# Mixer-0 norm and memory requests, and the state space's dq requests, issued in other places of a weight-streaming trunk

## The chip, the cores and the metric

One core of a Trainium2 chip runs the whole program. The metric is device time in microseconds; the kernel before takes 2868.22 us, the median of three runs (2866.78 to 2868.61).

## The reference

Two decoder layers over x of 256 tokens by 2048, batch 1, with 256 memory rows. Each layer is a token mixer, a cross-attention to the memory and a squared-ReLU MLP of width 8192, each on an RMS norm of x and added to x; a last RMS norm ends it. Mixer 0 is a gMLP, mixer 1 a complex-diagonal state space with a gated output. All is float32.

```python
def chunked_gmlp(h, w_in, b_in, ln_g, ln_b, w_s, b_s, w_out):
    z = jax.nn.gelu(h @ w_in + b_in, approximate=False)
    u, v = jnp.split(z, 2, axis=-1)
    v = layer_norm(v, ln_g, ln_b)
    v = v.reshape(bsz, seq // CHUNK, CHUNK, A_HEADS, A_HEAD_DIM)
    w = jnp.where(causal[None], w_s, 0)
    s = jnp.einsum('hts,bnshd->bnthd', w, v) + b_s   # one 128x128 matrix per head
    return (u * s.reshape(bsz, seq, A_WIDTH)) @ w_out

def s5_glu(h, w_in, lam, log_dt, bm, cm, d_skip, w_out, b_out):
    u = (h @ w_in).reshape(bsz, seq, B_GROUPS, B_GROUP)
    # per group: state s_t = lam_bar * s_(t-1) + b_bar u_t (64 complex), y = Re(c s) + d u
    y = jax.nn.gelu(y, approximate=False)
    val, gate = jnp.split(y @ w_out + b_out, 2, axis=-1)
    return val * jax.nn.sigmoid(gate)

# memory: k, v = rms_norm(mem, g_mem) @ w_kv, in both layers
```

## The kernel before

Weights are not resident: each matrix comes from HBM in chunks of 512 KB, 128 partitions by 1024 float32. `wload` (L118) requests a chunk on SP's queue into one of four `wraw` buffers. `split` (L101, L102) divides it into a rounded part `whi` (a ScalarE cast) and the remainder `wlo` (a VectorE subtraction), three buffers each. TensorE then takes twelve matmuls per chunk (L145 to L147): activation high part by `whi`, high by `wlo`, low by `whi`. Nearly all of TensorE's work has this form, or its transposed one (L163, L165).

Other work is put between the chunks by a plan. `at(d, fn)` runs a function d chunks later, `tick` at the end of each chunk runs what is due, and takes one step of the list `side` at every `every`-th chunk with a priority `lag` lower. A scheduler then sets each engine's order by priority; on the chip each engine works its list in that order, and a DMA request is an instruction of the engine that issues it. Buffers come from pools: a tile of a tag waits until the last reader of the buffer it takes is done.

The stages of the first mixer, `gmlp`: `features` loads x transposed in pieces (`memc`, two buffers), `zin(n)` makes one of eight column tiles of z with a bias row (`bc`, L111, one row broadcast to 128 partitions, 256 KB, requested on POOL's queue), the first four being v. `mixing` loads w_s as four pieces (`wsr`), masks them on POOL and splits them. `ln(j, t)` normalizes v: L362 subtracts the mean and multiplies by ln_g, L364 scales and adds ln_b. Each pair (ln_g, ln_b) is requested by `ln` at t = 0. b_in, ln_g, ln_b and w_s share the two buffers of the tag `bc`. `gate` and `turn` multiply by the mixed v and transpose. The output projection follows, and behind its first tile `mem_stats` loads the memory in four pieces on POOL's queue (L252, tag `memc`) and sums squares on ScalarE (L176), from which `rstd_mem` is made.

In the state space, `s5`, four column tiles n of u = h @ w_in are made. From each come chunk inputs (transposes, L894), own responses with `pq` (L908), carries (VectorE), and outputs with `dq` (L956) and `qq` (L962). The matrices pq, dq and qq were written to HBM by a preparation that runs beside the MLP of the first layer; they come back as tiles of 512 KB (L854) on POOL's queue, four of each per n, with four buffers per name. Before the first tile the four pq of n = 0 are requested; `follow(n)` puts the others into the plan.

## Time and profile before

| what | us |
|---|---|
| median of three runs | 2868.22 |
| profiled execution, own time | 2870.24 |
| its span, first to last instruction | 2868.5 |
| TensorE busy | 2818.8 (98%) |
| VectorE busy | 1831.0 (64%) |
| ScalarE busy | 1333.9 (47%) |
| POOL busy | 205.6 (7%) |

The mean granted clock of TensorE is 0.996 of full speed. In the rows below, PE is TensorE, DVE VectorE, ACT ScalarE, POOL GpSimd, SP the engine that only issues requests; a suffix q is a request put in a queue. Times are from the start of the span. A number in square brackets at a row's end is the idle time of that engine before the instruction, with what ended it. A lone time after a tile's name is the time from request to landing.

### The profile page before, as it was taken

How to read it: one execution, taken by the hardware profiler on the slowest of the kernel's cores; microseconds unless marked ns; L12 is line 12 of the kernel's file. 1: busy time of each engine (PE TensorE's matmuls, PEld its weight loads, DVE VectorE, ACT ScalarE, POOL GpSimd, SP SyncE). 2: the span in 40 equal slices, each digit the busy share in tenths (PEclk: the TensorE clock that was granted, in tenths of full speed). 3: DMA queues.
4: the chain of work that ended last, by engine and by line, in shares of the span. 5: the costliest groups of instructions: out<-in, count | busy, mean ns of one | idle time of the engine just before them, and what ended most of it. 6: DMA issues, size and time to landing. Idle time of an engine off the chain costs nothing.

```text
span 2868.5 us, 39577 instructions
## 1 busy us (share of the span) xinstructions
PE 2818.8 (98%) x15238; PEld 2362.5 (82%) x15238; DVE 1831.0 (64%) x2548; ACT 1333.9 (47%) x1714; POOL 205.6 (7%) x384
## 2 busy tenths in 40 slices
PE   8999999999999999999999999999999999999998
PEld 6778888888888888888877788888888888888886
DVE  5655655576778878787567567555556555555565
ACT  5444544444544444444555445444454444344443
POOL 1000000000022222222011000000000000000000
PEclk9999999999999999999999999999999999999999
DMA  7766656557677777777689866656566666666665
GB/s 260 221 197 190 200 174 177 176 171 231 197 216 211 225 222 214 220 221 212 217 248 273 233 203 212 184 173 185 169 187 187 192 190 189 192 186 191 190 189 154
DMA packets 180461, 579.55 MB, mean 202 GB/s; under 512 B 37440, under 2 KB 39664, under 8 KB 179504
## 3 DMA queue, kind: packets, MB, share of 16 engines
q1 hardware_dynamic: 140864, 509.67, 58.7%
q0 software_dynamic: 39264, 67.29, 8.6%
q8 instruction: 119, 1.95, 0.3%
q14 instruction: 70, 0.57, 0.1%
q10 hardware_dynamic: 144, 0.07, 0.0%
HBM read 553.88 MB, written 22.94 MB: 201 GB/s over the span
## 4 chain that ended last, share of the span: by engine, by line
PE 88%; DMA 5%; DVE 3%; issue 2%; ACT 1%; POOL 0%; SPq 0%; DVEq 0%; ACTq 0%; POOLq 0%
PE acc L163 23%; PE acc L165 12%; PE acc L146 8%; PE acc L570 8%; PE acc L147 8%; PE acc L569 8%; PE acc L145 8%; PE acc L568 8%; DVE wlo L102 1%; PE ps L504 1%; PE ps L448 1%; DMA wraw<-in_b_w_in 1%; DMA Kd<-kd 1%; PE ps L214 1%; DMA wraw<-in_a_w_in 1%
## 5 line engine op out<-in xcount | busy, mean ns | idle before, releaser
L102 DVE TENSOR_TENSOR wlo<-wraw,whi 128x1024 fp32r<-128x1024 f32 x952 | 1164.1, 1223 | 847.6 <-ACT whi L101 845.7
L101 ACT CAST whi<-wraw 128x1024 fp32r<-128x1024 f32 x952 | 1000.9, 1052 | 1290.8 <-PE acc L163 401.1
L163 PE MATMUL acc<-act,whi 128*128 128x512 f32 x3072 | 1083.0, 396 | 0.3 <-ACT whi L101 0.3
L165 PE MATMUL acc<-act,wlo 128*128 128x256 f32 x3072 | 865.0, 282 | 2.6 <-DVE wlo L102 2.6
L163 PEld LDWEIGHTS acc<-act,whi 128*128 128x128 f32 x3072 | 576.1, 188 | 133.5 <-issue 1.6
L165 PEld LDWEIGHTS acc<-act,wlo 128*128 128x128 f32 x3072 | 580.4, 189 | 7.9 <-DVE wlo L102 4.5
L145 PE MATMUL acc<-whi,act 128*128 128x512 f32 x1248 | 492.6, 395 | 12.7 <-ACT whi L101 11.2
L146 PE MATMUL acc<-wlo,act 128*128 128x512 f32 x1248 | 491.2, 394 | 12.4 <-DVE wlo L102 12.4
L147 PE MATMUL acc<-whi,act 128*128 128x512 f32 x1248 | 489.2, 392 | 0.3 <-DVE act L102 0.3
L569 PE MATMUL acc<-wlo,hh 128*128 128x512 f32 x992 | 389.0, 392 | 0.0
L568 PE MATMUL acc<-whi,hh 128*128 128x512 f32 x992 | 388.8, 392 | 0.0
L570 PE MATMUL acc<-whi,hl 128*128 128x512 f32 x992 | 388.6, 392 | 0.0
L146 PEld LDWEIGHTS acc<-wlo,act 128*128 128x128 f32 x1248 | 236.3, 189 | 64.8 <-DVE wlo L102 17.6
L145 PEld LDWEIGHTS acc<-whi,act 128*128 128x128 f32 x1248 | 235.7, 189 | 64.7 <-ACT whi L101 13.8
L147 PEld LDWEIGHTS acc<-whi,act 128*128 128x128 f32 x1248 | 236.2, 189 | 48.4 <-DVE act L102 0.7
L570 PEld LDWEIGHTS acc<-whi,hl 128*128 128x128 f32 x992 | 186.3, 188 | 40.3 <-issue 1.6
L569 PEld LDWEIGHTS acc<-wlo,hh 128*128 128x128 f32 x992 | 186.3, 188 | 40.2 <-issue 1.0
L568 PEld LDWEIGHTS acc<-whi,hh 128*128 128x128 f32 x992 | 186.3, 188 | 39.7 <-issue 0.4
L819 POOL DMA_DIRECT2D Kd<-kd x128 | 72.4, 581 | 188.8 <-issue 176.7
L101 ACT CAST hh<-r 128x512 fp32r<-128x512 f32 x64 | 39.5, 617 | 23.0 <-DVE r L534 22.8
L552 DVE SCALAR_TENSOR_TENSOR x<-acc,r,x 128x512 f32<-128x512 f32 x62 | 43.7, 746 | 8.6 <-PE acc L570 8.6
L176 ACT ACTIVATE junk<-x 128x512 f32<-128x512 f32 x56 | 35.3, 630 | 21.1 <-DVE x L545 13.5
(288 smaller groups left out, 1661.3 us busy)
## 6 DMA issues: line engine op xcount, KB each, us to landing
wraw<-in_f_w_up SPq DMA_DIRECT2D x256, 512.0 KB, 4.4
wraw<-in_f_w_down SPq DMA_DIRECT2D x256, 512.0 KB, 4.4
wraw<-in_a_w_in SPq DMA_DIRECT2D x64, 512.0 KB, 4.7
wraw<-in_x_w_q SPq DMA_DIRECT2D x64, 512.0 KB, 3.7
wraw<-in_x_w_k SPq DMA_DIRECT2D x64, 512.0 KB, 3.7
wraw<-in_x_w_v SPq DMA_DIRECT2D x64, 512.0 KB, 3.7
wraw<-in_x_w_o SPq DMA_DIRECT2D x64, 512.0 KB, 3.7
wraw<-in_b_w_out SPq DMA_DIRECT2D x64, 512.0 KB, 4.4
```

Source lines behind the costliest of these rows:

```text
L101: self.nc.scalar.copy(out=hi, in_=src)
L102: self.nc.vector.tensor_tensor(out=lo, in0=src, in1=hi.bitcast(F32), op=ALU.subtract)
L145: nc.tensor.matmul(out[t], ah[:, kt, sl], hi[:, kk, :], start=st, stop=False)
L146: nc.tensor.matmul(out[t], ah[:, kt, sl], lo[:, kk, :], start=False, stop=False)
L147: nc.tensor.matmul(out[t], al[:, kt, sl], hi[:, kk, :], start=False, stop=en)
L163: nc.tensor.matmul(acc[:, f, :], hi[:, kk, sl], both[:, kt].rearrange("p a s -> p (a s)"), start=st, stop=False, skip_group_check=True)
L165: nc.tensor.matmul(acc[:, f, 0:S], lo[:, kk, sl], ah[:, kt, :], start=False, stop=en, skip_group_check=True)
L552: nc.vector.scalar_tensor_tensor(out=xc, in0=acc[:, t, :], scalar=r2[:, t:t + 1], in1=xc, op0=ALU.mult, op1=ALU.add)
L568: nc.tensor.matmul(acc[:, t, :], ah[:, kt % 4, sl], hi[:, kk, :], start=st, stop=False)
L569: nc.tensor.matmul(acc[:, t, :], ah[:, kt % 4, sl], lo[:, kk, :], start=False, stop=False)
L570: nc.tensor.matmul(acc[:, t, :], al[:, kt % 4, sl], hi[:, kk, :], start=False, stop=en)
L819: nc.gpsimd.dma_start(out=self.Kd[q // 2][:, :, q % 2, t], in_=kd[32 * t:32 * t + 16])
```

## The change

The bias rows of `zin` get a tag of their own, `bz`, with two buffers, and are requested at the start of the column tile instead of at its activation. The x_t pieces and the memory pieces share a tag `u` of five buffers with the tiles u. `ln` no longer requests its rows: `affine(j)` does, the first ahead of all steps and each following one as a step of its own after pair j's second, with a step at every second chunk instead of every third. The memory pieces are requested on SP's queue behind a weight, one at every second chunk of the output projection's second tile, with the row statistics in a function of their own eight chunks in. In the state space the four dq of n = 0 are requested right behind the four pq of n = 0, and no longer from `follow(0)`.

```diff
--- before.py
+++ after.py
@@ -106,8 +106,8 @@
         a = self.act.tile([P, KT, 2, S], F32R, name="act")
         return a[:, :, 0, :], a[:, :, 1, :], a
 
-    def bc(self, pool, src):
-        t = pool.tile([P, NB], F32, name="bc")
+    def bc(self, pool, src, tag="bc", bufs=None):
+        t = pool.tile([P, NB], F32, name="bc", tag=tag, **({"bufs": bufs} if bufs else {}))
         self.nc.gpsimd.dma_start(out=t, in_=src.rearrange("(o n) -> o n", o=1).broadcast_to([P, NB]))
         return t
 
@@ -248,9 +248,17 @@
         nc = self.nc
         ss = self.new_ss()
         for j in range(NCH):
-            m = pool.tile([P, 2, NB], F32, name="memc")
-            self.tc.keep_in_program_order(nc.gpsimd.dma_start(out=m, in_=self.a["mem"][j]))
-            self.sumsq(m, ss, j)
+            def piece(j):
+                m = pool.tile([P, 2, NB], F32, name="memc", tag="u", bufs=5)
+                with self.tc.issue_after(self.fed):
+                    nc.sync.dma_start(out=m, in_=self.a["mem"][j])
+                self.sumsq(m, ss, j)
+
+            self.at(2 * j, lambda j=j: piece(j))
+        self.at(2 * NCH, lambda: self.mem_rows(ss))
+
+    def mem_rows(self, ss):
+        nc = self.nc
         self.rstd_mem = self.rstd(ss, "rstd_mem", self.const)
         self.rows_mem = self.const.tile([P, 2, P], F32, name="rows_mem")
         pt = self.ps([P, 2, P])
@@ -279,7 +287,7 @@
             ss = self.new_ss()
 
             def features(j):
-                xt = gp.tile([P, 4, S], F32, name="memc")
+                xt = gp.tile([P, 4, S], F32, name="memc", tag="u", bufs=5)
                 for h in range(0, 4, 2):
                     nc.sync.dma_start(out=xt[:, h:h + 2], in_=a["x_t"][j][:, h:h + 2])
                     if j == 0 and h == 0:
@@ -305,22 +313,21 @@
             bs = gp.tile([P, KT], F32, name="bs", bufs=1)
 
             def zin(n, out):
-                nonlocal rstd
+                b = self.bc(gp, a["a_b_in"][n * NB:(n + 1) * NB], "bz", 2)
                 acc = self.gemm_tok(hT, a["a_w_in"], n, raw=first)
                 if rstd is None:
                     self.flush()
                     self.lag = 100
                     for k in range(NCH):
                         self.at((1, 3, 4, 6)[k], lambda k=k: tokens(k))
-                    self.at(7, lambda: activate(n, out, acc))
+                    self.at(7, lambda: activate(n, out, acc, b))
                 else:
-                    activate(n, out, acc)
-
-            def activate(n, out, acc):
+                    activate(n, out, acc, b)
+
+            def activate(n, out, acc, b):
                 nonlocal rstd
                 if rstd is None:
                     rstd = self.rstd(ss, "rstd")
-                b = self.bc(gp, a["a_b_in"][n * NB:(n + 1) * NB])
                 for t in range(2):
                     nc.vector.scalar_tensor_tensor(out=out[:, t, :], in0=acc[:, t, :], scalar=rstd[:, t:t + 1],
                                                    in1=b, op0=ALU.mult, op1=ALU.add)
@@ -354,9 +361,10 @@
 
             lnb = {}
 
+            def affine(j):
+                lnb[j] = [self.bc(gp, a[k][j * NB:(j + 1) * NB]) for k in ("a_ln_g", "a_ln_b")]
+
             def ln(j, t):
-                if t == 0:
-                    lnb[j] = [self.bc(gp, a[k][j * NB:(j + 1) * NB]) for k in ("a_ln_g", "a_ln_b")]
                 lg, lb = lnb[j]
                 vc = v[:, t, j, :]
                 nc.vector.scalar_tensor_tensor(out=vc, in0=vc, scalar=mv[:, t, 0:1], in1=lg,
@@ -366,8 +374,12 @@
                 v4 = vc.rearrange("p (h d) -> p h d", h=4)
                 self.split(vh[:, 4 * j:4 * j + 4, t, :], vl[:, 4 * j:4 * j + 4, t, :], v4)
 
-            self.side += [lambda j=j, t=t: ln(j, t) for j in range(NCH) for t in range(2)]
-            self.every = 3
+            affine(0)
+            for j in range(NCH):
+                self.side += [lambda j=j: ln(j, 0), lambda j=j: ln(j, 1)]
+                if j + 1 < NCH:
+                    self.side += [lambda j=j: affine(j + 1)]
+            self.every = 2
             usT = self.new_act()
 
             def gate(j, u):
@@ -396,16 +408,15 @@
                     kt = 4 * j + 2 * hp
                     self.split(usT[0][:, kt:kt + 2, :], usT[1][:, kt:kt + 2, :], pt)
 
-            us = [gp.tile([P, 2, NB], F32, name="u", bufs=4) for _ in range(NCH)]
+            us = [gp.tile([P, 2, NB], F32, name="u", bufs=5) for _ in range(NCH)]
             for j in range(NCH):
-                if j == 3:
-                    self.every = 1
                 zin(j, us[j])
                 if j:
                     self.at(1, lambda j=j: gate(j - 1, us[j - 1]))
                     self.at(3, lambda j=j: turn(j - 1, us[j - 1]))
             self.at(2, lambda: gate(NCH - 1, us[NCH - 1]))
             self.at(4, lambda: turn(NCH - 1, us[NCH - 1]))
+            self.every = 1
             acc0 = self.gemm_tok(usT, a["a_w_out"], 0, kts=range(12), last=False)
             self.flush()
 
@@ -981,7 +992,8 @@
                 for i in range(4):
                     if n + 1 < NCH:
                         self.at(4, lambda i=i: fetch("pq", n + 1, i))
-                    self.at(6 + i // 2 * 2, lambda i=i: fetch("dq", n, i))
+                    if n:
+                        self.at(6 + i // 2 * 2, lambda i=i: fetch("dq", n, i))
                     self.at(6 + i // 2 * 2, lambda i=i: fetch("qq", n, i))
                 self.at(3, lambda: inputs(n))
                 self.at(4, lambda: own(n))
@@ -994,8 +1006,9 @@
                 self.at(15, lambda: outputs(n, 1))
                 self.at(17, lambda: features(n))
 
-            for i in range(4):
-                fetch("pq", 0, i)
+            for nm in ("pq", "dq"):
+                for i in range(4):
+                    fetch(nm, 0, i)
             for n in range(NCH):
                 acc = self.gemm_tok(hT, a["b_w_in"], n)
                 if n == 0:
```

On POOL, in the first mixer, these are the rows from the first norm pair to the last bias. Before (a_ln_g and a_ln_b are the norm's rows, a_b_in the bias, in_mem the memory):

```order
L111 DMA bc<-in_a_ln_g 128x512
L111 DMA bc<-in_a_ln_b 128x512
L111 DMA bc<-in_a_ln_g 128x512
L111 DMA bc<-in_a_ln_b 128x512
L111 DMA bc<-in_a_b_in 128x512
L111 DMA bc<-in_a_ln_g 128x512
L111 DMA bc<-in_a_ln_b 128x512
L111 DMA bc<-in_a_b_in 128x512
L111 DMA bc<-in_a_ln_g 128x512
L111 DMA bc<-in_a_ln_b 128x512
L111 DMA bc<-in_a_b_in 128x512 x2
L252 DMA memc<-in_mem 128x1024 x4
```

After:

```order
L111 DMA bc<-in_a_ln_g 128x512
L111 DMA bc<-in_a_ln_b 128x512
L111 DMA bc<-in_a_b_in 128x512 x4
L111 DMA bc<-in_a_ln_g 128x512
L111 DMA bc<-in_a_ln_b 128x512
L111 DMA bc<-in_a_ln_g 128x512
L111 DMA bc<-in_a_ln_b 128x512
L111 DMA bc<-in_a_b_in 128x512
L111 DMA bc<-in_a_ln_g 128x512
L111 DMA bc<-in_a_ln_b 128x512
L111 DMA bc<-in_a_b_in 128x512
```

Before, four biases stand ahead of the first row shown (two of them ahead of the mixing weights); now it is two, and four more follow the first norm pair at once. The memory requests are gone from this queue, and no bias stands between the second and the third norm pair.

On POOL, at the head of the state space, where the first matrices are read back (Kd, Pd, Qd are the HBM copies). Before:

```order
L854 DMA pq<-Pd_5524 128x1024
L854 DMA pq<-Pd_5525 128x1024
L854 DMA pq<-Pd_5526 128x1024
L854 DMA pq<-Pd_5527 128x1024
L919 MEMSET vv 128x2x16
L854 DMA dq<-Kd_5556 128x1x1024
L854 DMA qq<-Qd_5540 128x1024
L854 DMA dq<-Kd_5557 128x1x1024
L854 DMA qq<-Qd_5541 128x1024
L854 DMA dq<-Kd_5558 128x1x1024
```

After:

```order
L865 DMA pq<-Pd_5524 128x1024
L865 DMA pq<-Pd_5525 128x1024
L865 DMA pq<-Pd_5526 128x1024
L865 DMA pq<-Pd_5527 128x1024
L865 DMA dq<-Kd_5556 128x1x1024
L865 DMA dq<-Kd_5557 128x1x1024
L865 DMA dq<-Kd_5558 128x1x1024
L865 DMA dq<-Kd_5559 128x1x1024
L930 MEMSET vv 128x2x16
L865 DMA qq<-Qd_5540 128x1024
L865 DMA qq<-Qd_5541 128x1024
L865 DMA qq<-Qd_5542 128x1024
```

The four dq stand directly behind the four pq, in front of the memset of vv; the four qq stay behind it, and the pairs of dq and qq no longer alternate.

On ScalarE, at the first mixer's end, the sums of squares of the memory pieces (junk,ss<-memc) and the weight casts (whi) around them. Before:

```order
L327 ACTIVATE u<-u 128x1024
L101 CAST whi<-wraw 128x1024
L176 ACTIVATE junk,ss<-memc 128x512 x2
L101 CAST whi<-wraw 128x1024
L176 ACTIVATE junk,ss<-memc 128x512 x2
L101 CAST whi<-wraw 128x1024
L101 CAST act<-ps 128x2x256 x2
L176 ACTIVATE junk,ss<-memc 128x512 x3
L101 CAST whi<-wraw 128x1024
L176 ACTIVATE junk,ss<-memc 128x512
L101 CAST whi<-wraw 128x1024 x4
```

After:

```order
L176 ACTIVATE junk,ss<-memc 128x512 x2
L101 CAST whi<-wraw 128x1024 x4
L176 ACTIVATE junk,ss<-x 128x512 x2
L101 CAST whi<-wraw 128x1024
L223 ACTIVATE act<-ps,gcol 128x256 x2
L176 ACTIVATE junk,ss<-memc 128x512 x2
L223 ACTIVATE act<-ps,gcol 128x256 x2
L176 ACTIVATE junk,ss<-memc 128x512
L101 CAST whi<-wraw 128x1024
L176 ACTIVATE junk,ss<-memc 128x512 x2
L101 CAST whi<-wraw 128x1024
L176 ACTIVATE junk,ss<-memc 128x512
```

Three casts lay between the first sum of squares and the last, and now seven; the sums stand later, in the output projection, between activations of the next norm.

## Rows read from the trace of the kernel before

**Rows 1.** The page: engines' busy time, and a costly group of instructions.
```profile
PE 2818.8 (98%) x15238; PEld 2362.5 (82%) x15238; DVE 1831.0 (64%) x2548; ACT 1333.9 (47%) x1714; POOL 205.6 (7%) x384
...
L146 PE MATMUL acc<-wlo,act 128*128 128x512 f32 x1248 | 491.2, 394 | 12.4 <-DVE wlo L102 12.4
```

**Rows 2.** Timeline of ScalarE, an undisturbed stretch: start, length, instruction, idle before.
```profile
97.92 1.05 ACT L101 CAST whi<-wraw 128x1024 fp32r<-128x1024 f32 x1 [1.67 <-PE acc L147]
```

**Rows 3.** Windows: busy time of the engines, granted clock, DMA share, GB/s.
```profile
0.00:25.00 25.00, 15.15 (x52) 10.97 (x53) 13.19 (x23) 14.99 (x25) 2.42 (x9) 1.00 0.79 275
60.00:70.00 10.00, 8.68 (x37) 6.40 (x35) 6.43 (x9) 4.62 (x6) 3.73 (x6) 1.00 0.70 220
130.00:160.00 30.00, 23.67 (x100) 18.35 (x99) 20.76 (x26) 12.73 (x15) 3.81 (x8) 0.94 0.57 174
160.00:190.00 30.00, 25.92 (x112) 20.42 (x111) 15.78 (x31) 15.50 (x28) 1.53 (x3) 0.94 0.71 232
1366.00:1394.00 28.00, 28.00 (x130) 23.27 (x129) 15.27 (x17) 13.40 (x19) 1.72 (x5) 1.00 0.81 272
1441.00:1480.00 39.00, 33.17 (x149) 26.31 (x148) 21.23 (x39) 18.72 (x34) 5.90 (x11) 1.00 0.99 275
1460.00:1490.00 30.00, 24.17 (x160) 18.73 (x159) 13.06 (x16) 17.43 (x34) 2.12 (x4) 0.94 0.95 301
1500.00:1510.00 10.00, 8.33 (x48) 6.51 (x50) 9.57 (x27) 7.32 (x17) 0.00 (x0) 1.00 0.59 167
1530.00:1545.00 15.00, 12.42 (x56) 10.16 (x55) 11.19 (x17) 10.27 (x24) 0.00 (x0) 0.89 1.03 254
```

**Rows 4.** Timeline of VectorE in the layer norm.
```profile
129.46 0.75 DVE L362 SCALAR_TENSOR_TENSOR v<-v,mv,bc 128x512 f32<-128x512 f32 x1 [2.65 <-DMA bc<-in_a_ln_g]
...
151.23 0.75 DVE L364 SCALAR_TENSOR_TENSOR v<-v,rv,bc 128x512 f32<-128x512 f32 x1 [4.65 <-DMA bc<-in_a_ln_b]
```

**Rows 5.** The broadcast rows (tile bc) before 260: request to landing.
```profile
DMA to landing us min/median/max: 4.3/5.3/8.5
```

**Rows 6.** Timeline of POOL in the layer norm.
```profile
123.63 0.54 POOL L111 DMA_DIRECT2D bc<-in_a_ln_g  x1 [2.66 <-DVE v L364]
...
145.73 0.54 POOL L111 DMA_DIRECT2D bc<-in_a_ln_b  x1 [7.02 <-DVE v L362]
```

**Rows 7.** Timeline of ScalarE at the memory rows.
```profile
176.75 0.63 ACT L176 ACTIVATE junk<-memc 128x512 f32<-128x512 f32 x1 [2.76 <-DMA memc<-in_mem]
```

**Rows 8.** Tile memc (x_t and memory pieces) before 260: request to landing.
```profile
DMA to landing us min/median/max: 3.0/5.9/9.2
```

**Rows 9.** Timeline of POOL in the state space.
```profile
1441.24 0.65 POOL L854 DMA_DIRECT2D dq<-Kd  x1 [73.51 <-DVE x L552]
```

**Rows 10.** DMA issues of 1362 to 1376: tiles, queue, KB each, median us to landing.
```profile
wraw<-in_f_w_down SPq DMA_DIRECT2D x5, 512.0 KB, 6.5
pq<-Pd POOLq DMA_DIRECT2D x4, 512.0 KB, 10.2
```

**Rows 11.** DMA issues of 1440 to 1480.
```profile
wraw<-in_b_w_in SPq DMA_DIRECT2D x12, 512.0 KB, 10.7
dq<-Kd POOLq DMA_DIRECT2D x4, 512.0 KB, 21.0
```

**Rows 12.** Timeline of TensorE in the state space, the first tile's transposes.
```profile
1479.18 1.30 PE L894 MATMUL ps<-ident,u 128*128 128x128 f32 x8 [4.13 <-ACT u L883]
```

**Rows 13.** The mixing weights (tile wsr): counts and durations; request to landing.
```profile
L101 ACT CAST wsh<-wsr x4: 620/620/622, 56.6 to 69.5; 128x512 fp32r<-128x512 f32 x4
L102 DVE TENSOR_TENSOR wsl<-wsr,wsh x4: 680/692/693, 57.2 to 70.4; 128x512 fp32r<-128x512 f32 x4
...
DMA to landing us min/median/max: 3.8/4.0/4.4
```

**Rows 14.** Timeline of SP in the start.
```profile
15.91 1.38 SPq L118 DMA_DIRECT2D wraw<-in_a_w_in  x3
```

**Rows 15.** Timeline of ScalarE in the start.
```profile
22.07 1.04 ACT L101 CAST whi<-wraw 128x1024 fp32r<-128x1024 f32 x1 [2.27 <-DMA wraw<-in_a_w_in]
```

## The prediction

> **What bounds the kernel now.** The page comes first: TensorE holds work for 98% of the span, while VectorE has 64% and ScalarE 47% [rows 1]. So the kernel is a stream of weight chunks through TensorE, and the change can pay only where TensorE stands still or runs at a lower clock. A chunk is twelve matmuls; in an undisturbed stretch ScalarE's cast of one takes 1.05 us and stands 1.67 us before it [rows 2], so chunks come every 2.72 us and matmuls start 0.227 us apart, while the page gives each 394 ns because they overlap [rows 1]. A gap shown as idle is therefore about 0.17 us longer in lost time than the number beside it.
>
> The windows view shows where TensorE stands still [rows 3]. The loss of a stretch is its length less the busy time, plus 0.17 per gap, plus busy time times (1 minus the granted clock); a mean of 0.94 is a mixture of full speed and the lower of the two levels.
> - 60 to 70 (the mixing weights are cast): 1.32 idle, three gaps, full clock: 1.8 us.
> - 130 to 160 (layer norm of the first mixer): 6.33 idle, four gaps, clock 0.94 (1.4): 8.4 us.
> - 160 to 190 (statistics of the memory rows): 4.08 idle, three gaps, clock 0.94 (1.6): 6.2 us.
> - 1460 to 1490 (state space, first tile): 5.83 idle, four gaps, clock 0.94 (1.5): 8.0 us.
> - 1500 to 1510 (second tile): 1.67 and 0.17: 1.8 us. 1530 to 1545 (third tile): 2.58 idle, 0.17, clock 0.89 (1.4): 4.2 us.
>
> Together 30 us, about 1% of the time. The timelines of the engines then give the cause of each. In the layer norm TensorE's second matmul of a chunk waits for VectorE's wlo, the costliest such wait of the page [rows 1], and VectorE, which takes its instructions in order, stands before the norm's first or second operation for a weight row that was requested late: 2.65 us in the earliest of four such places and 4.65 in the last [rows 4]. These rows take 4.3 to 8.5 us from request to landing [rows 5]; POOL requests them only when an operation on an earlier row of the tag is over [rows 6]. At the memory rows ScalarE stands twice before a sum of squares, 2.76 us the second time [rows 7], until the DMA of the rows lands, up to 9.2 us after its request [rows 8]; the weight cast is behind it in its queue. In the state space POOL waits 73.51 us for the last MLP down projection's residual and then issues eight 512 KB requests, four dq and four qq, back to back [rows 9]; from then on the DMA engines are busy for 0.99 of 39 us and still move only 275 GB/s [rows 3], a weight chunk, which took 6.5 us to land beside the four pq requests [rows 10], takes 10.7 [rows 11], and at the end the transposes of the first tile stand 4.13 us [rows 12].
>
> **The change, part by part.** The sum is made against the profiled execution, 2870.24 us (span 2868.5 and 1.7 around it), which lies 2.0 above the median of 2868.22.
>
> *Mixing weights.* w_s no longer shares buffers with b_in, so POOL has no wait ahead of its first two loads, and select, cast and subtract of all four pieces move from 51 to 70 us to the first 25. The 1.8 us go: -1.8. In the start the same four casts (0.62) and four subtracts (0.69) [rows 13] stand ahead of the weight casts 4 and 7. TensorE is already idle for 9.85 of the first 25 us [rows 3], waiting on transfers, and that covers the 5.2 us of added work as long as the data are there. Two things pull apart: 1 MB more must land there (at the 275 GB/s of this stretch [rows 3], 3.8 us, the upper end with a little wait, +4), and the fourth weight request, now issued at 15.91 because SP stood behind an x_t piece without a buffer [rows 14], can go out with five buffers at once; the 2.27 us that ScalarE waits for that chunk [rows 15] may go, of which I allow 1.5. I take +0.8, the middle being 1.2 and the nearer row being ScalarE's.
>
> *Layer norm.* Norm pair j+1 is now its own step ahead of pair j's use, and b_in has buffers of its own. In POOL's order b_in goes in front and the norm rows follow each other. Pair 2's weight, requested at 123.63 [rows 6] behind a b_in on the same tag, goes when that b_in went, some 3 us earlier. The last pair waits for operations of earlier pairs that, counted along the changed order, end near 131.7 and 134, where the last bias was requested at 145.73 [rows 6]. With the worst landing of 8.5 us they are there at 140.2 and 142.6; VectorE stood ready for the last bias at 151.23 - 4.65 = 146.6 [rows 4]. So all four waits fall. What is late next is the second pair, still bound by its buffers, and the steps of the norm now come every second chunk instead of every third. I leave 0.8 (from 0 to 2.1, a fourth of the stretch's 8.4, if one of the four waits comes back): -7.6.
>
> *Memory rows.* Four requests leave POOL's queue for SP's, spaced over six chunks of the output projection, into five buffers; counted along ScalarE's order, the sums of squares follow their requests by two chunks for the first piece and four to six for the others. The stretch has 0.71 of the DMA in use at 232 GB/s [rows 3]. Each 512 KB piece delays the weights behind it on the queue by some 1.7 us (at the 301 GB/s that flowed in 1460 to 1490 [rows 3]), and there are two chunks, 5.4 us, for each: 1.05 MB of weights and 0.52 of rows in 5.4 us are 290 GB/s, just under what flowed there. What is left over is 0.2 (0 to 1.4, a third of the idle time now): -6.0. The Trainium skill ("Trainium Kernel Development and Optimization", Key Constraints) says that requests issued by SP, ScalarE and POOL run on the same 16 DMA engines, so that another issuer only saves issue time. By that the move buys nothing in bandwidth, and the saving rests on spacing and buffers alone; the sum here counts none for the queue.
>
> *State space, first tile.* The four dq requests now stand behind the four pq, ahead of the vv memset, and their buffers wait only for TensorE work of the preparation: issue near 1367.6 instead of 1441 to 1445. At 1440 four requests are left of eight, 2.1 MB instead of 4.2. The weights need one chunk in 2.72 us, 193 GB/s. The 8.0 us go, but for 0.8 (0 to 3; the second tile, with no such burst, still loses 1.8): -7.2.
>
> *Third tile.* TensorE's transposes for it stand ten matmuls (2.3 us) later in the changed order; against the 2.75 us gap most of it goes and with it part of the lower clock: -2.8 (-4.2 to 0). The second tile's place is unchanged: 0.
>
> *New burst at 1366.* Four pq requests alone bring the weights' landing to 6.5 us [rows 10], and TensorE has no gap in 1366 to 1394 [rows 3]. Eight requests at 1441 brought 10.7 [rows 11] and the 8.0 us. The new burst is eight again, but with the fast pq first (they land in 10.2 us, dq in 21.0 [rows 10, 11]), in a stage where ScalarE has less beside the casts. Ends: 0 (as with pq alone) and +6 (three quarters of what eight cost at 1441). I take +3. In 1440 to 1480 twelve weight chunks were requested beside eight requests of POOL, of the same 512 KB, so neither queue held the other up for long [rows 11]. The Trainium skill ("DMA: Bandwidth & Descriptors", Queues, rings and completion order) states that each engine takes the queues with work in turn, packet by packet. By it dq's 2.1 MB would take half of 275 GB/s for 15 us, the weights fall behind by 15 x (1 - 137/193) = 4.4 us, and with 6.5 us or so of landing that is what stopped TensorE at 1441: the upper half of the range. The trace agrees as far as the counts go: twelve chunks against eight pieces, not one queue first.
>
> **Sum:** -1.8 + 0.8 - 7.6 - 6.0 - 7.2 - 2.8 + 3 = -21.6. 2870.2 - 21.6 = 2848.6, less the 2.0: 2846.6 us.
>
> **Rivals.**
> 1. The burst only moves. dq at 1367 stops TensorE as it did at 1441, and what the third tile loses stays. For it: the weights' landing of 10.7 under eight requests. Against: pq alone shows no gap, and here half the bytes move 75 us ahead. The state space then gives nothing: -21.6 + 7.2 + 2.8 - 3 = -14.6 from the gMLP, 2853.6.
> 2. Another request is late in the first mixer: ScalarE stands before the memory pieces again, now that weights and rows share one queue, or VectorE before the second norm pair. For it: 290 GB/s asked against 301 seen at best. Against: four to six chunks of lead for three pieces, and two, 5.4 us, for the first against a median landing of 5.9 [rows 8], with ScalarE 1.67 us ahead at each cast [rows 2]. Half of the 13.6 us returns: 2853.4.
> 3. Slower. ScalarE stands in the start before the casts of w_s: the second pair is requested only after the first is subtracted, and each stands ahead of weight casts. If each of the four pieces lands as late as the slowest memory row (9.2 us [rows 8]), one after the other, the price is 4 x (9.2 + 0.62 + 0.69) = 42.0 us, less the 9.85 that TensorE stands there anyway: 32.2, and the sum is -22.4 + 32.2 = +9.8: 2878.0. It decides once the start costs over 22.4 us. Against: w_s landed in 4.0 us where it is loaded now [rows 13], and its requests are issued two at a time.
> 4. The edit does not free dq: its requests wait for the residual, as now, and hold POOL. Nothing but POOL is behind them, so the state space is as before and the gMLP gains: 2853.6 again.
>
> **How the numbers follow.** Forecast 0.62, with its own range 2840 to 2853; rivals 1 and 4 together 0.19; rival 2 0.10; rival 3 0.04; several small things at once that eat it 0.05, at 2860 to 2868. For the range I take the low end from the terms' better ends (start -1.5, burst 0, third tile -4.2: 2840, and 2 more for the clock) and the high end from rivals 1, 2 and 4 with the start at +4 and 4 us more of leftover: 2838 to 2862. What a measurement can tell from no change is 0.2%, 5.7 us: faster needs less than 2862.5. Faster 0.88, within 0.2% 0.08, slower 0.04.
>
> **What would show it.** Right: in 130 to 190 no DVE wait on a norm row and no ScalarE wait on memory rows above 1 us, TensorE busy above 29.5 of each 30; dq issued near 1367; the first tile's transposes waiting under 1.5 us; weights landing in 8 to 11 us around 1375 to 1390 with at most two gaps. Wrong: a gap in 1370 to 1395 of more than 6 us in sum (rival 1), or a start whose 25th microsecond holds fewer than 48 matmul records against 52 [rows 3] (rival 3).

## The result and the profile after

| | before | after |
|---|---|---|
| median, us | 2867.5 (4 runs, 2866.42 to 2868.61) | 2849.49 (4 runs, 2847.75 to 2852.07) |
| ratio to before | 1 | 0.9938, 95% interval 0.9921 to 0.9955 |
| profiled execution, us | 2870.24 | 2848.29 |
| its span, us | 2868.5 | 2846.5 |

The change makes the kernel 18.0 us faster by the medians and 22.0 by the two profiled executions. The forecast was 2846.6, in a range of 2838 to 2862. One run of a later kernel (the last but one below) took 4682.58 us at a granted clock of 0.556 and is left out of its median.

The windows of after, in the columns of [rows 3]. The stretches from 1346 on are shifted by some 20 us against before.

```profile
0.00:25.00 25.00, 15.04 (x50) 10.69 (x51) 15.32 (x25) 15.35 (x26) 7.15 (x16) 1.00 0.89 307
60.00:70.00 10.00, 10.00 (x45) 8.29 (x45) 5.53 (x7) 4.26 (x5) 0.00 (x0) 1.00 0.77 216
130.00:160.00 30.00, 29.03 (x138) 24.04 (x137) 21.30 (x27) 14.06 (x16) 1.07 (x2) 1.00 0.74 223
160.00:190.00 30.00, 30.00 (x143) 25.16 (x142) 16.58 (x19) 12.72 (x14) 0.00 (x0) 1.00 0.59 173
1346.00:1374.00 28.00, 28.00 (x128) 23.06 (x127) 12.77 (x14) 12.26 (x17) 4.76 (x9) 1.00 1.01 270
1374.00:1390.00 16.00, 14.25 (x62) 10.50 (x61) 9.50 (x12) 8.69 (x15) 0.00 (x0) 1.00 0.88 238
1441.00:1471.00 30.00, 29.81 (x195) 24.45 (x194) 18.10 (x26) 19.04 (x36) 2.10 (x4) 1.00 0.70 229
1481.00:1491.00 10.00, 8.34 (x111) 6.23 (x109) 7.75 (x13) 6.35 (x15) 2.08 (x4) 1.00 0.70 199
1506.00:1521.00 15.00, 11.49 (x51) 8.65 (x50) 12.68 (x21) 9.00 (x21) 0.00 (x0) 0.88 1.02 245
```

The three stretches of the first mixer, which lost 1.8, 8.4 and 6.2 us, now lose 0, 1.1 and 0, and the clock is whole again. The memory rows no longer fall into the third of them: they are requested from 204.93 to 220.63 and summed from 210.8 on, and nothing is lost there. TensorE's work in the start is unchanged (15.04 busy, against 15.15), with 307 GB/s instead of 275. The first state space tile (1441 to 1471) loses 0.2 where it lost 8.0. Two things are on the other side: a new loss at 1374 to 1390, 1.75 us idle, and the third tile (1506 to 1521), which is idle 3.51 us where it was 2.58 [rows 3]. The first tile's transposes, which waited 4.13 us in [rows 12]:

```profile
1456.56 1.09 PE L905 MATMUL ps<-ident,u 128*128 128x128 f32 x8 [0.19 <-ACT u L894]
```

The four requests of dq on POOL in after, where [rows 9] has 1441.24 and 73.51 us of waiting; then the DMA issues of 1350 to 1382 in after, beside [rows 10, 11].

```profile
1348.31 1.87 POOL L865 DMA_DIRECT2D dq<-Kd  x3
1350.89 0.58 POOL L865 DMA_DIRECT2D dq<-Kd  x1 [0.71 <-DMA Pd<-po]
```

```profile
wraw<-in_f_w_down SPq DMA_DIRECT2D x9, 512.0 KB, 11.9
dq<-Kd POOLq DMA_DIRECT2D x2, 512.0 KB, 32.0
```

dq is requested at once, and in the MLP the weights now land as late (11.9 us) as they did at 1441 (10.7).

To see where the 22.0 us come from I added, over all neighbouring starts of TensorE's matmuls, what goes beyond the usual distance, for each stretch of both traces. 26 to 130: 2.4 before, 0 after. 130 to 260: 14.7 and 1.1. 1300 to 1400: 0 and 2.5. First tile: 7.3 and 0.4. Second: 1.8 and 1.8. Third: 4.1 and 5.3. The start: 5.9 and 6.1. Between 520 and 1300, which the change does not touch, 4.1 and 2.6. The whole is 44.3 and 23.8, 20.5 us of the 22.0. Each count is of one execution. In the traces of the other runs, counted the same way, a stretch with the same code differs by one to five us, so a difference of a microsecond or two in one stretch says little by itself.

### The profile page after: what moved, and what is told of

It reads as the page before. It is cut to its first block, busy times and chain, and to the rows that moved or that the text cites. A ratio compares the mean times of both kernels' runs of the same rounds, so it can differ in the third digit from the quotient of the medians.

```text
span 2846.5 us, 39576 instructions
## 1 busy us (share of the span) xinstructions
PE 2811.6 (99%) x15238; PEld 2359.5 (83%) x15238; DVE 1830.3 (64%) x2548; ACT 1333.4 (47%) x1714; POOL 204.0 (7%) x380
## 4 chain that ended last, share of the span: by engine, by line
PE 92%; DMA 3%; DVE 2%; ACT 1%; issue 1%; SPq 0%; POOL 0%; DVEq 0%; ACTq 0%; POOLq 0%
PE acc L163 25%; PE acc L165 13%; PE acc L146 9%; PE acc L145 9%; PE acc L147 9%; PE acc L581 8%; PE acc L580 8%; PE acc L579 8%; PE ps L515 1%; DMA wraw<-in_f_w_down 1%; PE ps L459 1%; DVE wlo L102 1%; PE ps L214 1%; DMA wraw<-in_b_w_in 1%; DMA wraw<-in_f_w_up 1%
## 5 line engine op out<-in xcount | busy, mean ns | idle before, releaser
L830 POOL DMA_DIRECT2D Kd<-kd x128 | 72.4, 580 | 178.9 <-issue 166.7
```

What stands on the lines that cost most here:

```text
L830: nc.gpsimd.dma_start(out=self.Kd[q // 2][:, :, q % 2, t], in_=kd[32 * t:32 * t + 16])
```

## The experiments

Ratios are to the kernel before, run on the same chip (medians of 2867.5 to 2868.1 there).

**The first mixer's part alone.** after without the state space edit:

```diff
-            for nm in ("pq", "dq"):
-                for i in range(4):
-                    fetch(nm, 0, i)
+            for i in range(4):
+                fetch("pq", 0, i)
...
-                    if n:
-                        self.at(6 + i // 2 * 2, lambda i=i: fetch("dq", n, i))
+                    self.at(6 + i // 2 * 2, lambda i=i: fetch("dq", n, i))
```

> The whole change without its state space edit: the four dq of the first tile are requested with the qq again, as before. My theory: the first mixer and the state space give their gains independently. By the trace of after, TensorE lost 17.1 us less than before between 26 and 260 us; so 2867.5 - 16 = 2851.5 (2849 to 2854), and the state space shows the old picture: first tile's transposes stand about 4 us, weights land in 10 to 13 us. Rival: the state space carries the gain, as dq stands apart from qq; then this comes out at 2857 or above.

2853.88 us, ratio 0.9955 (0.9940 to 0.9969). The first tile's transposes wait as before, and weights land in 11.3 us:

```profile
1462.65 1.09 PE L905 MATMUL ps<-ident,u 128*128 128x128 f32 x8 [3.91 <-ACT u L894]
```

**The state space's part alone.** The same edit the other way round, made in the kernel before.

> The kernel before with the state space edit alone: the four dq of the first tile requested right behind the four pq. My theory: the first tile's 7 us go and 2.5 us come at the new burst beside the MLP, and the third tile keeps its loss; 2867.5 - 4 = 2863.5 (2861 to 2866). Rival: the state space pays as forecast, with the third tile (10 us less there, 3 at the burst): 2860.5 or lower. Second rival: the burst moved and nothing is gained: 2867.

2865.13 us, ratio 0.9991 (0.9981 to 1.0001): a gain that timing alone hardly separates from none. The trace shows both sides of it: the first tile's loss is gone, and near 1395 TensorE now loses 5.4 us in sum, most of it in front of the MLP's last transposes:

```profile
1394.79 0.33 PE L214 MATMUL ps<-ident,x 128*128 128x128 f32 x1 [2.54 <-DVE x L552]
```

The two parts add up: 0.45% and 0.09% against 0.62% of the whole, inside the intervals. Most of the gain is the first mixer's.

**Memory rows on POOL, all at one point, into five buffers.**

```diff
...
-            self.at(2 * j, lambda j=j: piece(j))
-        self.at(2 * NCH, lambda: self.mem_rows(ss))
...
+            m = pool.tile([P, 2, NB], F32, name="memc", tag="u", bufs=5)
+            self.tc.keep_in_program_order(nc.gpsimd.dma_start(out=m, in_=self.a["mem"][j]))
+            self.sumsq(m, ss, j)
```

> The changed kernel with the memory rows requested as before, all four at one point on POOL's queue and their sums of squares at once, but into the five shared buffers instead of two. Theory spacing: the requests in one burst are what made ScalarE stand before the sums, so a good part of the loss of before (6 us between 160 and 190) is back: 2849.5 + 4 = 2853.5 (2851 to 2856). Theory buffers: the loss came from two buffers that made the last two requests wait for the first sums; with five the loss is 1 us at most: 2850.

2850.48 us, ratio 0.9939 (0.9920 to 0.9958). The window 160 to 190 of this run, and the four requests on POOL:

```profile
160.00:190.00 30.00, 30.00 (x143) 25.16 (x142) 17.06 (x20) 12.57 (x13) 0.53 (x1) 1.00 0.65 210
```

```profile
149.85 0.53 POOL L252 DMA_DIRECT2D memc<-in_mem  x1
158.63 0.54 POOL L252 DMA_DIRECT2D memc<-in_mem  x1 [8.25 <-ACT whi L101]
182.77 0.53 POOL L252 DMA_DIRECT2D memc<-in_mem  x1 [23.60 <-ACT whi L101]
201.37 0.53 POOL L252 DMA_DIRECT2D memc<-in_mem  x1 [18.07 <-ACT junk L176]
```

TensorE is never idle in the window, and the gain is kept on POOL's queue: the new queue did not make it. Whether the spacing did is not shown, because the four requests did not come as a burst. As the five buffers came free they went out over 51 us, and the sums of squares stand at 199.6 to 206.9, where they stood at 166.7 to 178.3 before the change, so that ScalarE waits 0.72 us for one piece at most.

**Mixing weights late.** One tag, so that they wait for the biases' buffers:

```diff
-                wr = gp.tile([P, 4, P], F32, name="wsr", tag="bc", bufs=2)
+                wr = gp.tile([P, 4, P], F32, name="wsr", tag="bz", bufs=2)
```

> The changed kernel with the mixing weights on the bias tag, so that they wait for the biases' buffers as before and are masked and split near 50 to 70 us. My theory: the 2.4 us of TensorE between 60 and 70 come back (in part, since biases and norm rows no longer share the tag), and the start gains nothing, as it lost nothing: 2851.5 (2849 to 2854). Rival: the casts in the start cost as much as they save; then the first 26 us lose 2 us less and the time stays at 2849.5.

2853.07 us, ratio 0.9953 (0.9938 to 0.9968). Between 26 and 130 us 2.6 us are lost again, of which

```profile
87.44 0.50 PE L146 MATMUL acc<-wlo,act 128*128 128x512 f32 x1 [1.51 <-DVE wlo L102]
```

is the largest. The pieces are requested later here than before the change (59.02 to 78.93, against 51.45 to 64.66). The start loses 6.6 us, against 6.1 in after and 6.7 to 8.3 in the nine other runs with the hoist. So the hoist is worth its 2.4 us; that it costs the start nothing is not shown.

**The burst spaced.** The first tile's dq on SP's queue:

```diff
...
-            for nm in ("pq", "dq"):
-                for i in range(4):
-                    fetch(nm, 0, i)
+            def ahead_dq(i):
+                with tc.issue_after(self.fed):
+                    fetch("dq", 0, i, nc.sync)
+
+            for i in range(4):
+                fetch("pq", 0, i)
+                self.at(8 + 3 * i, lambda i=i: ahead_dq(i))
```

> The changed kernel with the four dq of the first tile on SP's queue behind the 8th, 11th, 14th and 17th weight of the state space's input projection (about 1430 to 1455), instead of behind pq in one burst beside the MLP. My theory: the loss of 2.5 us near 1375 goes, the weights there land as before the change (7 us at most), and the four pieces, one in 8 us, cost nothing: 2847 (2844.5 to 2849). Rival: dq costs its transfer wherever it stands, now beside qq of 1423 and pq of 1459: a gap of 2 us or more appears between 1430 and 1470 and the time stays at 2849.5 or rises to 2853.

2848.07 us, ratio 0.9932 (0.9917 to 0.9946), not to be told from after. Both expectations are half right: nothing is lost near 1375, and 3.6 us are lost between 1400 and 1480, with the first tile's transposes waiting again:

```profile
1455.42 1.88 PE L905 MATMUL ps<-ident,u 128*128 128x128 f32 x8 [2.29 <-ACT u L894]
```

The first weight behind a single dq lands in 11.7, 12.0, 10.6 and 8.1 us. Between 1432 and 1438, with nothing of POOL's queue under way, a 4 KB packet of SP's queue takes 349 ns. So it isn't the number of requests alone: dq is a slow transfer, on either queue.

**dq from plain rows** (the same bytes from the copy of qq):

```diff
-                    t = load(bass.AP(tensor=kd.tensor, offset=kd.offset,
-                                     ap=[[P, T], [(2 * T - 1) * P, 16], [1, T * P]]), nm, [P, T * P])
+                    t = load(self.Qd[4 * n + i].rearrange("l p r n -> (l p) (r n)"), nm, [P, T * P])
```

> The changed kernel with every dq tile read from the HBM copy of qq (512 KB in plain rows, no overlap) in place of the overlapping windows of Kd; so the state space's result is left out, the bytes and the requests are the same. Theory volume: eight requests on POOL's queue beside the weights take their share whatever they read; weights still land in about 12 us near 1365, TensorE loses 2 to 2.5 us there, the time stays within 2 us of after (2849.5). Theory pattern: the overlapping windows are slow to read; then POOL's eight requests land within 22 us instead of 33, weights land in under 9 us, no gap between 1365 and 1395, and tiles 2 to 4 lose less as well: 2841 to 2846.

2845.18 us, ratio 0.9923 (0.9908 to 0.9937): no gap of TensorE between 1300 and 1400. DMA issues of 1350 to 1382 and the window of the same stretch:

```profile
wraw<-in_f_w_down SPq DMA_DIRECT2D x12, 512.0 KB, 5.6
dq<-Qd POOLq DMA_DIRECT2D x4, 512.0 KB, 16.9
```

```profile
1350.00:1382.00 32.00, 32.00 (x151) 26.66 (x150) 18.95 (x22) 16.65 (x26) 2.23 (x5) 1.00 0.86 330
```

Weights in 5.6 us instead of 11.9, with 330 GB/s in the stretch. Between 1363 and 1380 a 4 KB packet takes 163 ns on POOL's queue, against 326 in after, and weights' packets 181 against 284: while dq is read, everybody's packets are slow. How dq is read costs more than that eight requests stand together.

**Which property of the read?** Three reads of the same 512 KB from the copy of qq, each with one property of dq's windows; only the pattern changes (each run has one of the last three lines, the first of them as it stood in after):

```diff
-                    kd = self.Kd[4 * n + i]
+                    kd = self.Qd[4 * n + i]
...
+                                     ap=[[P, T], [(2 * T - 1) * P, 16], [1, T * P]]   # windows
+                                     ap=[[0, T], [T * P, 16], [1, T * P]]             # rows eight times
+                                     ap=[[15 * T * P + P, T], [T * P, 16], [1, T * P]]  # rows off 512 bytes
```

> The changed kernel with dq read from the HBM copy of qq, but with the very windows of Kd (4 KB each, starting 512 bytes apart, 16 rows of 7.5 KB: 120 KB of memory for 512 KB read). The state space's result is left out. If the windows are what is slow: as after, 4 KB packets of POOL's queue take about 330 ns between 1365 and 1380 and weights land in 12 us. If it is the tensor Kd (where it lies, how it was written): 160 ns and under 8 us, as with plain rows of qq.

> The changed kernel with dq read from the HBM copy of qq: 16 rows of 4 KB, each row read for eight partitions, all starting at multiples of 4 KB (64 KB of memory for 512 KB read). The state space's result is left out. If reading the same small piece of memory many times is what is slow: packets take 330 ns or more, weights land in 12 us or more. If only windows that start off the 4 KB grid are slow: 160 ns and no gap of TensorE between 1345 and 1395.

> The changed kernel with dq read from the HBM copy of qq: 128 nearly separate rows of 4 KB (488 KB of memory for 512 KB read) whose start is moved on by 512 bytes for each 16 partitions, as in the windows of Kd. The state space's result is left out. If starts off the 4 KB grid are slow: about 330 ns a packet and weights at 12 us. If the overlap is what is slow: 160 ns and weights under 8 us.

All three are slow: weights land in 13.0, 12.2 and 13.4 us, POOL's packets take 404, 371 and 405 ns, one execution each of 2849.89, 2851.45 and 2855.75 us. DMA issues of 1350 to 1382 of the third:

```profile
wraw<-in_f_w_down SPq DMA_DIRECT2D x9, 512.0 KB, 13.4
dq<-Qd POOLq DMA_DIRECT2D x4, 512.0 KB, 33.9
```

None of my properties is the cause by itself: rows that start on the 4 KB grid are slow, and rows that hardly overlap are slow. What the three share with dq, and plain rows do not, is an outermost count of 8 in the source's pattern (8 times 16 rows of 1024, where a plain read has 128 rows).

**Outermost count 16.** The partitions of dq in the order (c, j), with u and pq stored to match; first in after, then in the kernel before.

```diff
-                                     ap=[[P, T], [(2 * T - 1) * P, 16], [1, T * P]]), nm, [P, T * P])
+                                     ap=[[(2 * T - 1) * P, 16], [P, T], [1, T * P]]), nm, [P, T * P])
...
-                u = sp.tile([P, 8, T, 16], F32, name="u", bufs=1)
+                u = sp.tile([P, 8, 16, T], F32, name="u", bufs=1)
```

> The changed kernel with the rows of dq in another order: partition (c, j) instead of (j, c), so that the outermost count of the read is 16 instead of 8; u, pq and the tile that makes Pd are stored in the same order, so the result is that of the reference. The bytes, the windows and the requests are as in after. Theory outermost count: the three slow reads of the last job have an outermost count of 8 and the fast ones (qq, pq, plain rows) of 128; with 16, packets take 160 ns as with plain rows, weights land in under 8 us near 1365, no gap there: 2845 (2842 to 2848), unless the strided writes of u and pq cost DVE more than 0.2 us each. Theory small memory: windows of 120 KB are slow however they are split; then 330 ns, 12 us, and 2849.5.

2860.27 us, ratio 0.9975 (0.9966 to 0.9985): 11 us slower than after. Its DMA issues of 1350 to 1382, and its group of VectorE's u between 1400 and 1640, with that of after (1390 to 1630) behind it:

```profile
wraw<-in_f_w_down SPq DMA_DIRECT2D x11, 512.0 KB, 8.2
pq<-Pd POOLq DMA_DIRECT2D x4, 512.0 KB, 7.9
dq<-Kd POOLq DMA_DIRECT2D x4, 512.0 KB, 19.7
...
L891 DVE TENSOR_TENSOR u<-acc,rstd 32x256 f32<-32x256 f32 x32 | 20.4, 639 | 2.8 <-ACT u L894 1.8 <-PE acc L147 0.5
```

```profile
L891 DVE TENSOR_TENSOR u<-acc,rstd 32x256 f32<-32x256 f32 x32 | 13.4, 419 | 1.3 <-PE acc L147 0.5 <-ACT u L894 0.2
```

The read is better: 235 ns a packet against 326, weights in 8.2 us against 11.9, 0.4 us lost near 1375 against 2.5. But the strided stores of u take 639 ns instead of 419 on VectorE (and 482 instead of 352 on ScalarE), and they stand in front of each tile's transposes:

```profile
1491.46 1.97 PE L905 MATMUL ps<-ident,u 128*128 128x128 f32 x8 [3.60 <-ACT u L894]
```

Over the whole state space (1400 to 1650) the loss rises from 10.2 to 16.5 us. My bound of 0.2 us a write was passed by 0.02 only, and 32 of them on a path without slack were enough for that. Between 520 and 1300, where Pd is made, the loss rises from 2.6 to 6.8, but the next run has the same edit there and loses 2.4, so this part is not shown to be the new order's, and its cause stays open.

> The kernel before with the new order of dq's rows alone: dq stays where it was, eight requests at 1441. Theory outermost count: most of the state space's loss goes without any move: weights land in 8 us at most, the first tile's transposes wait under 2 us (4.13 before), and the time falls by 5 to 9 us, 2859 to 2863, more than the move alone gave (2865.1). Theory small memory: no change, 2867.9 (within 2 us).

2874.09 us, ratio 1.0028 (1.0019 to 1.0037). The same two sides again: weights between 1440 and 1480 land in 8.3 us against 10.7 [rows 11], and the transposes of the first three tiles wait 3.6 to 4.9 us; over the state space the loss rises from 16.1 to 21.4 us. The forecast of 2859 to 2863 left u's price out.

**Outermost count 16 without strided stores.** Eight requests for each dq, one for each shift:

```diff
...
+                    for j in range(T):
+                        nc.gpsimd.dma_start(out=t[16 * j:16 * j + 16], in_=bass.AP(
+                            tensor=kd.tensor, offset=kd.offset + j * P, ap=[[(2 * T - 1) * P, 16], [1, T * P]]))
...
```

The cut leaves out a priority that moves the first memsets of vv and the first qq forward.

> The changed kernel with each dq requested as eight pieces, one for each shift: 16 rows of 4 KB, so the outermost count of every read is 16; u and pq keep their order, so VectorE writes what it wrote in after. The windows and the bytes are the same; POOL issues 128 requests for dq in place of 16 (about 0.55 us each, 18 us a tile at most, POOL being idle there), and the first memsets of vv and the first qq are held ahead of the next pq by a priority. Theory: with the outermost count of 16 the weights land in 8 to 11 us near 1365 as in the run with the other row order, TensorE loses under 1 us there, and nothing is lost to VectorE: 2846.5 (2844 to 2849). Rival: 32 requests in a row are late themselves, dq lands after qq of its tile and the outputs wait, or POOL's queue holds pq of the next tile back: a wait of L967 of 2 us or more and 2852.

2864.79 us, ratio 0.9989 (0.9980 to 0.9998), 15 us slower than after. Near 1375 nothing is lost (weights in 8.6 us), but the rival was right about POOL's queue, and more than it said. POOL's timeline:

```profile
1356.48 0.48 POOL L878 DMA_DIRECT2D dq<-Kd  x1 [1.59 <-DMA pq<-Pd]
1360.01 0.48 POOL L878 DMA_DIRECT2D dq<-Kd  x1 [3.04 <-DMA pq<-Pd]
1364.03 0.48 POOL L878 DMA_DIRECT2D dq<-Kd  x1 [3.54 <-DMA pq<-Pd]
...
1520.06 0.49 POOL L878 DMA_DIRECT2D dq<-Kd  x1 [3.38 <-DMA qq<-Qd]
```

With eight requests under way, POOL waits until an older one has landed. With 40 requests a tile this queue becomes the pace of pq, qq and vv; TensorE stands 7.03 us before a chunk at 1549 for ScalarE's u. Which of the late requests makes u late there I did not take apart. A packet of POOL's queue takes 287 ns between 1363 and 1380, and one of the weights 238, so an outermost count of 16 by itself does not bring 163.

## Why the prediction was right, and where not

The stages that were to gain did gain: the late rows no longer stand in front of VectorE and ScalarE as they did, nor the late matrices in front of the first tile. One small term, the third tile, did not come. Of the signs set down beforehand, dq went out at 1348 (1367 less the shift), the first tile's transposes wait 0.19 us, and the two signs of being wrong did not come. Three were missed by a little: a norm row is waited for 2.37 us and not under 1, TensorE has 29.03 of the 30 us from 130 and not 29.5, and weights beside dq land in 11.9 us and not in 8 to 11.

*Mixing weights*: forecast -1.8 and +0.8, measured -2.4 and +0.2. The +0.2 is one pair of traces: the start loses 4.5 to 5.9 us in the three traces with the old first mixer and 6.1 to 8.3 in the ten with the new one, about 2 us more on average, which is inside my upper end of +4; whether the casts or the transfers cost it is not shown. POOL did wait for the second pair until 20.39, and the price of the slower rival (22 us) never came near.

*Layer norm and memory*: forecast -13.6 together, measured -13.6 (14.7 before; the two other traces with the old first mixer lose 13.5 and 9.7 there). Of the four waits on norm rows one is left, behind which TensorE stands 0.97 us:

```profile
134.98 1.41 DVE L370 SCALAR_TENSOR_TENSOR v<-v,mv,bc 128x512 f32<-128x512 f32 x2 [2.37 <-DMA bc<-in_a_ln_g]
```

It stands at the last pair, whose weight was requested at 128.76 and needed at 132.6. I had set its landing against the time at which VectorE was ready before, 146.6, though a step at every second chunk makes VectorE ready sooner. The second pair, where I expected the next wait, costs VectorE 1.05 us at 112.94 and TensorE nothing. For the memory rows the queue is worth nothing, as the sum had it. Which of the two reasons given, spacing or buffers, does it is not shown, since the five buffers spaced the requests by themselves when they went out on POOL.

*First tile*: forecast -7.2, measured -6.9.

*New burst*: forecast +3, measured +2.5, and 5.4 with the edit alone (3.6 and 3.4 in the runs with the memory rows on POOL and with the mixing weights late, which have the same burst). The size was right, the reason half right. I took dq's lateness at 1441 for queueing, eight pieces beside the weights. The plain rows show that eight equal requests need not stop TensorE. What I had under the eye was 275 GB/s at a DMA share of 0.99 [rows 3], where the start moved as much at a share of 0.79: full engines, few bytes. The Trainium skill ("DMA: Bandwidth & Descriptors", Why a DMA increments its semaphore by 16 and not by 1) states that a request is spread over the largest number of engines, up to 16, that divides the slowest dimension of both its patterns, with an exception for some copies that GpSimd requests. By that dq goes to 8 engines, unless it falls under the exception, and plain rows and pq to 16. The runs agree with it as far as they go: slow at an outermost count of 8 in all four patterns, better at 16. Which engine served a packet the trace does not tell, but it counts packets of 4 bytes. On SP's queue the 984 weights and other requests come to 16 of them each, and each of the four dq of the spaced run to 8, which would be eight engines if each that takes part sends one. On POOL's queue a dq with a count of 8 comes to 144, and with 16, or from plain rows, to 16. Why a packet takes twice as long at a count of 8 is not shown; a number of engines is not a packet's time. At 16 a packet still takes 235 ns and not 163; whether the small memory of the windows is the rest stays open, since no run had them with a larger count. At a count of 8 its size made no difference: 404 ns with 120 KB and 405 with 488 KB.

*Third tile*: forecast -2.8, measured +1.2 in this pair, and no change over all: in the old place the transposes' tile loses 4.1 and 4.4 us (before, and the first mixer's part alone), in the new one 3.1 to 5.3 in the four runs with this state space. This step failed. I read from the order that the transposes stand ten matmuls later, and took the gap in front of them for a fixed time that the ten matmuls fill. The gap was made by VectorE, which has 12.68 of 15 us there, and a weight that lands late (ScalarE's cast waits 2.79 us for it); with transposes later, the wait stands at the weight's wlo, and then at the transposes again:

```profile
1515.82 0.50 PE L146 MATMUL acc<-wlo,act 128*128 128x512 f32 x1 [1.77 <-DVE wlo L102]
1518.56 1.04 ACT L101 CAST whi<-wraw 128x1024 fp32r<-128x1024 f32 x1 [2.79 <-DMA wraw<-in_b_w_in]
1520.93 1.97 PE L905 MATMUL ps<-ident,u 128*128 128x128 f32 x8 [1.74 <-ACT u L894]
```

Added up, the parts give -19.0 against the -21.6 of the forecast, and the third tile alone makes 4.0 us of difference, which smaller terms offset in part. That the whole count is -20.5 is luck by 1.5 us, which lie between 520 and 1300, where nothing was changed. Profile to profile it is -22.0, by the medians -18.0; the four runs of after spread over 4.3 us, those of before over 2.2, and of the profiled pair the one of before lies above all its timed runs, the one of after near the low end.

*Rivals*: the first (the burst moves and the state space gives nothing) came nearest in its mechanism. The first mixer's part alone is 4.4 us slower than the whole change by the medians, so it was not nothing, but the state space edit in itself is worth about 0.1%, hardly clear of nothing.

## What to carry to other kernels

When an engine that works in order stands before a late request, look first at which buffer the request waits for: here tags of their own, shared buffers and earlier requests gave 14 of the 18 us, and for the memory rows the old queue did as well as the new one once there were five buffers. Before a burst is moved, compare its GB/s with its DMA share; a transfer that fills the engines and moves little is slow in itself, and will be slow beside whatever it is moved to. And look for what makes a gap in the engine that feeds the instruction: here moving the transposes back did not take the gap away.

## What the runs showed of the hardware

A read of 128 rows of 4 KB with an outermost count of 8 in its pattern took 326 to 405 ns a packet and slowed the other queue's packets to 272 to 302 ns (163 and 181 with plain rows), whether its rows overlapped or not. With a count of 16 over the same windows it took 235 ns, and 287 as eight requests. A read with a count of 8 came to 8 packets of 4 bytes on SP's queue, where every other request came to 16, and to 144 on POOL's queue. POOL's queue held at most eight requests under way. A VectorE store of 256 elements in 32-byte steps took 639 ns against 419 in 4-byte steps.
